# One five-column matmul per row tile in the experts' token fetch, and a small reduction on VectorE

## The chip, the core and the metric

The kernel runs on one core of one Trainium2 chip. The metric is the device time of that core in microseconds (us). The kernel before takes 3927.16 us, the median of three runs (3925.86 to 3930.93).

The engines are named as in the profile: PE is TensorE's matmul side and PEld its weight load, DVE is VectorE, ACT is ScalarE, POOL is GpSimd, SP is SyncE, which here only issues DMAs.

## The reference, cut to what matters

The program is two blocks one after the other. The first block has two layers; each ends in a mixture of experts over 1024 tokens of 1024 features. Every expert chooses its own 128 tokens:

```
aff = softmax(xn @ w_router)                  # [1024 tokens, 16 experts]
g, idx = top_k(aff.T, 128)                    # each expert's 128 tokens and their affinities
xg = xn[idx]                                  # their rows, [16, 128, 1024]
hid = silu(xg @ w_gate) * (xg @ w_up)         # 1024 -> 768
y = (hid @ w_down) * g                        # 768 -> 1024
h = h + zeros.at[idx].add(y)
```

All of it is in float32 accuracy: a matrix product is done as three products of a high and a low half.

## The kernel before

**The stage.** Each of the two layers runs the 16 experts in a stage of about 460 us (955 to 1420 us and 2102 to 2575 us). An expert's three matrices (9 MB) come from DRAM in six units of 128 x 3072: two each for gate, up and down. A unit is loaded by SP to `mwr`, its high half `mwh` is made on ACT (L130, three pieces of 128 x 1024), and its low half `mwl = mwr - mwh` on DVE or, for every sixth unit (down's first), on POOL (L134). There are three `mwh` and three `mwl` buffers, so a unit's halves can be made when the unit three places earlier has been used up on PE. PE multiplies 48 times for gate, 48 for up and 36 for down. Down's first unit feeds 18 matmuls, six to each piece of 1024; the third and fourth of each six read `mwl`.

**Around an expert.** `fetch` (L1190) finds the expert's tokens: DVE builds a one-hot matrix `oh` (tokens x slots, eight row tiles, L1195), PE multiplies it with the columns `lrhs` (token number in two parts, affinity in three), and the sums stand in a PSUM tile `idx`. The two parts of the token number are added in PSUM by a second matmul on the same one-hot tile. DVE then casts the number to an integer (`idx`, L1202) and adds the affinity's three parts (`gsc`, L1210), and POOL gathers the rows (`xg`, L1212). `tokens` (L1215) transposes the rows on PE in two groups of four (`xgT`), of which ACT and DVE make `xgh` and `xgl`. After gate and up, `hid` is formed by ACT (Silu, L1255) and DVE (L1256), transposed in two groups of three (`hT`) and split into `hh` and `hl`. `down` (L1269) is done one expert later; its result is scaled on ACT (`ye`, L1275) and scattered by POOL.

**PSUM.** Gate, up and down have two banks each. Everything small, that is `idx`, both `xgT` and both `hT`, shares two banks (tag `tp`): a third such tile waits until one of the two was read.

**The order.** It is written by a scheduler at build time, which plays the program through with its own estimates of time and puts the instructions of each engine in the order in which they came ready there (`high_priority` blocks first). On the chip every engine runs its list strictly in that order. The lists of the two layers' expert stages are the same.

Of the kernel before, what the change touches and what calls it, by code (L numbers as in the profile page):

```python
# [20 lines left out]
P = 128  # L21
# [55 lines left out]
class Kern:  # L77
# [10 lines left out]
    # -- small helpers --  # L88
# [9 lines left out]
    @contextmanager  # L98
    def staged(self, side=None, n=2048, bufs=2):
        """The ring that weights come in through: tiles [128, n]."""  # L100
        with self.pool("stage", bufs, side=side) as self.stage:
            self.stage_n = n
            yield

    def raw(self, k, n):
        """[128, k, n] of that ring."""
        return self.stage.tile([P, self.stage_n], F32, name="raw", tag="raw")[:, 0:k * n].rearrange("p (k n) -> p k n", k=k)
# [5 lines left out]
    def banks(self, ordered=False, **spec):  # L113
        """PSUM for one phase: tag=(banks a tile, tiles); ordered: in this order, else in that of use."""
# [21 lines left out]
    def rsqrt(self, v, n):  # L136
        """1/sqrt of v [P, n] (positive), on VectorE."""
# [16 lines left out]
    def bcast_row(self, pool, vec, n, name):  # L154
        """A DRAM vector [n] on every partition."""
        t = pool.tile([P, n], F32, name=name)
        self.nc.sync.dma_start(out=t, in_=vec.rearrange("(o n) -> o n", o=1).broadcast_to([P, n]))
        return t

    def columns(self, pool, rows, name):  # L160
        """DRAM row blocks [(n, 128) APs] -> [128, sum n], one column a row."""
# [19 lines left out]
    def to_T(self, xn, hi, lo, t, tags=("tp", "tp")):  # L181
        """xn [128 t, 1024 d] -> columns t of hi/lo [128, 8, T]."""
# [7 lines left out]
    def mm3(self, ps, wh, wl, uh, ul, kt, n=1024, first=True, last=True):  # L190
        """ps [M, n] += sum over k tiles of w^T u; w(k) gives [K, M] APs, u(k) gives [K, n] APs."""
# [8 lines left out]
def load_w(K, pool, W, c0, n, kt, name, lo_eng="dve", tag=None):  # L200
    """W [kt*128, C] columns c0:c0+n -> hi, lo [128, kt, n]."""
# [12 lines left out]
def weight_blocks(K, pool, W, c0, n, lo_eng="dve", bufs=2, tag=""):  # L214
    """Yields hi, lo [128, 8, 128] of the 128-column blocks of W [1024, C] from column c0."""
# [13 lines left out]
def range_reduced_sin(K, pool, out, z, b, fr, n):  # L229
    """out = sin(fr * (z + b)) for z [64, n] in PSUM."""  # L230
# [15 lines left out]
class Mixed:  # L246
    """A layer's transposed output in DRAM, in pieces of 128 rows and 512 tokens."""
# [5 lines left out]
    def store(self, k, src):  # L253
        """Rows k * 128 .. + 128 from src [128, T]."""
# [3 lines left out]
    def load(self, out, k0, k1, t):  # L258
        """out [128, KT, 128], its entries k0 .. k1: those row blocks of token tile t."""
# [7 lines left out]
class Hyena:  # L267
    """Layer 0's mixer: projections, implicit filters, long convolutions as real DFT products."""
# [25 lines left out]
    def load_forward(self, pool):  # L294
        """The matrices of the forward transform alone."""
# [3 lines left out]
    def load_inverse(self, pool):  # L299
        """Those of both transforms and those of the inverse one."""  # L300
# [7 lines left out]
    # folds of a [128, 1025] row block z (z[:, 1024] = 0); cos and sin sources may differ  # L308
# [33 lines left out]
    def to_freq_in(self, pool, f0, f1):  # L342
        """Folded rows of two channel tiles -> transposed hi/lo pieces, (class, j) -> [128, 512] views."""
# [15 lines left out]
    def forward(self, zt, emit):  # L359
        """emit(index 0..7, psum [128, 512] = C|S of 256 channels)."""  # L360
# [33 lines left out]
    def filter_mlp(self, sn, h2s):  # L394
        """The filters' hidden features [feature, t], hi over lo."""
# [26 lines left out]
    def stream_block(self, cb, wh, wl, uh, ul, wk):  # L422
        """Projected stream block cb [128 c, t] with its three-tap convolution, to DRAM."""
# [10 lines left out]
    def filters(self, h2s, zp, inverse):  # L434
        """The spectra of all filters, to DRAM; meanwhile the inverse transform's matrices."""
# [136 lines left out]
    def conv_out(self, g, o, z, Y, gate, wk, mixT):  # L572
        K, nc, mh, ml, ih, il = self.K, self.nc, self.mh, self.ml, self.ih, self.il
        V = nc.vector
        for ci in range(2):
# [21 lines left out]
            # unfold  # L597
# [81 lines left out]
def first_norm(K, pool, src, g, hi, lo, dst=None, each=None, bufs=8, gp=None, x0=None):  # L679
    """rms_norm of DRAM rows src [n*128, D] with gain g, transposed and split (and to DRAM dst); each(t) follows tile t.  # L680

    x0: the first 128 rows, if they are on chip."""
# [31 lines left out]
def accurate_exp(K, pool, x, n):  # L714
    """In-place exp of x [P, n] <= 0 on VectorE (float32 accuracy)."""
# [16 lines left out]
class Mem:  # L732
    """Memory cross-attention of one layer."""
# [7 lines left out]
    def load(self, pool):  # L741
        """Keys and values that were left in DRAM."""
# [12 lines left out]
    def kv(self, pool, mt, wp, mem):  # L755
        """Keys and values from the memory (hi, lo); pool holds what the attention needs."""
# [29 lines left out]
    def key_pair(self, pool, ps, n, name):  # L786
        """Two heads' K^T (64 partitions each) in PSUM -> [hi; hi] and [lo; lo] a head."""
# [13 lines left out]
    def queries(self, pool, w, uh, ul, tag="mm"):  # L801
        """qs [hi; lo] (the other way round for the odd head) of two heads; w their columns' hi, lo."""
# [11 lines left out]
    def attend(self, wk, mixT, row0, pair, qs, tg, pk=None):  # L814
        """Heads 2 pair and 2 pair + 1, token tiles 2 tg and 2 tg + 1."""
# [24 lines left out]
def scores(K, out, qs, k2, kl2):  # L840
    """out [128 t, n keys] = q k^T from the stacked halves."""
# [9 lines left out]
def softmax_rows(K, pool, ps, G):  # L851
    """ps [128, N] scores of G softmaxes a row -> probabilities [128, N] float32."""
# [16 lines left out]
def exp_rows(K, pool, ps, sm):  # L869
    """ps [128, n] scores of one softmax a row -> their exponentials under the row's maximum; the sums to sm."""  # L870
# [8 lines left out]
def columns_to_rows(K, ps, v):  # L879
    """ps [64, n * 128] (PSUM): column j of v [128, n] along the free dim, the same on each partition."""  # L880
# [4 lines left out]
def pT(K, prob, ph, pl, tt, pool=None, off=()):  # L885
    """prob's transpose, split, as columns of token tile tt of ph, pl; blocks of four key tiles in off are split from a copy on Pool."""
# [16 lines left out]
def out_heads(K, pool, ph, pl, kv, dst, tag="tp", sums=None):  # L903
    """dst (DRAM [64, n]) = V^T P^T (over sums [128, n / 128]); kv lists (index of ph, [hi | lo] values [128, 128])."""
# [26 lines left out]
class Moe:  # L931
# [14 lines left out]
    def out_weights(self, pool, rp, W, ks):  # L946
        """Row tiles ks of W, split."""
# [9 lines left out]
    def mix_out(self, mixT, W, xsrc):  # L957
        """h = x + mix @ W, its norm, the affinities, a token tile at a time.

        The mixer's last rows come last; the pools lie where its memory is free early."""  # L960
# [31 lines left out]
    def route_tile(self, wk, h, t, project):  # L992
        """Token tile t: h, its norm and its affinities; the last tile in halves, for the sake of what waits for it.

        The logits are four sums over two row blocks each, side by side in the array's columns."""
# [44 lines left out]
    def affinities(self, t):  # L1040
        """Those of token tiles t, t + 1 from the scaled logits."""
# [12 lines left out]
    def fall(self, src, s):  # L1054
        """Bitonic rows [n, 2 s] of src in falling order."""
# [12 lines left out]
    def larger(self, top, n):  # L1068
        """The larger halves of rows i and n + i of top [2 n, 128], sorted."""
# [7 lines left out]
    def joined(self, a, b):  # L1077
        """The 128 largest of two falling lists, sorted."""
# [4 lines left out]
    def pair_list(self, q):  # L1083
        """The 128 largest affinities a row of token tiles 2 q, 2 q + 1, in falling order: halves are sorted, then joined."""
# [17 lines left out]
    def route(self, pool):  # L1102
        """Slots [128 t, 8, 16] (minus 1000; 0 or more where a token is not chosen) and the matrices that list them."""
# [3 lines left out]
        with K.pool(name="rt", bufs=1, side="right") as rp:  # L1107
# [34 lines left out]
            # token number in two exact parts, affinity in three  # L1142
# [4 lines left out]
            nc.gpsimd.tensor_copy(out=rhs[:, :, :, 0], in_=iot[:, 0])  # L1147
# [3 lines left out]
            for j in range(3):  # L1151
                V.tensor_copy(out=rhs[:, :, :, 1 + j], in_=cur)
                if j < 2:
                    V.tensor_tensor(out=res, in0=cur, in1=rhs[:, :, :, 1 + j], op=OP.subtract)
                    cur = res
# [7 lines left out]
    def load(self, W, k0, n, c):  # L1163
        """Rows p * kt + k0 .. + n of every partition's run of W [kt * 128, c], split."""
# [13 lines left out]
    def accumulate(self, ps, parts, xh, xl, W, c):  # L1178
        """ps [128, c] = x W over all the rows of W, 3072 elements of a partition's run at a time."""
# [10 lines left out]
    def fetch(self, wk, xk, e):  # L1190
        """Expert e's token numbers, affinities and token rows."""
# [6 lines left out]
        for t in range(NT):  # L1198
            K.mm(ps[:, 0:4], oh[:, t], self.rhs[:, t, e, 0:4], t == 0, False)
            K.mm(ps[:, 0:1], oh[:, t], self.rhs[:, t, e, 4:5], False, t == NT - 1)  # L1200
        idx = wk.tile([P, 1], I32, name="idx", tag="idx", bufs=4)
        V.tensor_copy(out=idx, in_=ps[:, 0:1])  # L1202
# [1114 lines left out]
```

## Time and profile before

| | |
|---|---|
| median of three runs | 3927.16 us |
| span of the profiled execution | 3930.2 us |
| highest of the three runs | 3930.93 us |
| PE, DVE, ACT, POOL busy | 91%, 73%, 52%, 40% of the span |
| chain that ended last | PE 53%, DVE 13%, POOL 7%, ACT 4%, DMA 3% |
| mean granted TensorE clock | 0.953 of 2.4 GHz |
| DMA | 603.62 MB, mean 154 GB/s |

The profiled execution's span is 3.0 us above the median and 0.7 us under the highest of the three runs. In the profile's rows a group such as `mwl<-mwr,mwh` names the tile written and the tiles read; `x3` means three instructions in a row; a bracket tells how long the engine was idle before and what ended that idle time.

### The profile page before, as it was taken

To read this page: it belongs to the slowest core of one execution; us is meant where nothing else is said; L and a number is where in the kernel's file an instruction comes from. 1 tells how busy PE (TensorE), PEld (TensorE's weight loads), DVE (VectorE), ACT (ScalarE), POOL (GpSimd) and SP (SyncE) were. 2 spreads that over 40 slices of the span, in tenths; PEclk is the share of its full clock that TensorE was granted. 3 is DMA by queue.
4 is the path that set the end of the run, shared out by engine and by line. 5 is a ranking of instruction groups with operands and counts; after the bars stand their busy time and mean duration, and the time that the engine had idled before them with its cause. 6 is when DMAs were issued, how large, how long until landed. Compare 5 with 4: busy or idle time off the path is not lost.

```text
span 3930.2 us, 52452 instructions
## 1 busy us (share of the span) xinstructions
PE 3572.0 (91%) x19469; PEld 3034.8 (77%) x19469; DVE 2882.4 (73%) x4751; ACT 2047.2 (52%) x3063; POOL 1562.0 (40%) x1227
## 2 busy tenths in 40 slices
PE   7997999994999979899886999989998999999998
PEld 6885878773988979777765988978786877778777
DVE  6547878778888789777687988776476667765675
ACT  4333532233767754789634767745584245545430
POOL 2004745532443422244342543313351049774710
PEclk9998999897999999999997999999999999999999
DMA  4223333463999951000355999951114312222251
GB/s 152 96 82 109 116 129 114 132 233 143 363 356 353 369 178 37 11 10 12 100 203 216 367 348 353 350 151 53 38 39 133 99 56 91 70 75 76 91 176 65
DMA packets 205690, 603.62 MB, mean 154 GB/s; under 512 B 23095, under 2 KB 114073, under 8 KB 179834
## 3 DMA queue, kind: packets, MB, share of 16 engines
q1 hardware_dynamic: 193737, 558.58, 39.3%
q0 software_dynamic: 11696, 41.69, 4.1%
q8 instruction: 154, 2.52, 0.3%
q14 instruction: 103, 0.84, 0.1%
HBM read 503.59 MB, written 96.60 MB: 153 GB/s over the span
## 4 chain that ended last, share of the span: by engine, by line
PE 53%; DVE 13%; POOL 7%; ACT 4%; DMA 3%; issue 2%; SPq 0%; DVEq 0%; ACTq 0%; POOLq 0%
PE out L176 9%; PE gate L176 8%; PE xbc L176 5%; PE up L176 5%; PE down L176 5%; DVE mwl L134 2%; PE ov L176 2%; PE z L176 2%; PE gs L176 2%; PE pT L125 1%; PE as L176 1%; PE qk L176 1%; PE xr L176 1%; POOL csr L2048 1%; POOL csr L2047 1%
## 5 line engine op out<-in xcount | busy, mean ns | idle before, releaser
L134 DVE TENSOR_TENSOR mwl<-mwr,mwh 128x1024 fp32r<-128x1024 f32 x468 | 611.2, 1357 | 54.0 <-ACT mwh L130 52.9
L130 ACT ACTIVATE mwh<-mwr 128x1024 fp32r<-128x1024 f32 x576 | 562.7, 1050 | 48.6 <-PE up L176 24.5
L134 POOL TENSOR_TENSOR mwl<-mwr,mwh 128x1024 fp32r<-128x1024 f32 x108 | 295.0, 2759 | 311.2 <-ACT mwh L130 281.0
L915 POOL TENSOR_TENSOR oh<-oh,oh 64x256 f32<-64x256 f32 (+1 forms) x56 | 55.1, 984 | 401.2 <-ACT oh L914 386.7
L134 DVE TENSOR_TENSOR gpl<-pT,gph 128x512 fp32r<-128x512 f32 x168 | 110.5, 684 | 43.6 <-ACT gph L130 32.6
L1480 DVE SCALAR_TENSOR_TENSOR cv<-xbc,sdcols,cv 128x1021 f32<-128x1021 f32 (+2 forms) x72 | 91.9, 1276 | 65.8 <-ACT cv L1477 65.5
L125 PE MATMUL pT<-ident,prob 128*128 128x128 f32 x896 | 127.3, 278 | 13.5 <-DVE gpl L134 8.0
L873 DVE TENSOR_REDUCE mx<-gs 128x1 f32<-128x1024 f32 x96 | 116.8, 1218 | 30.9 <-PE gs L176 30.5
L176 PE MATMUL gate<-mwh,xgl 128*128 128x384 f32 x512 | 137.1, 349 | 0.3
L176 PE MATMUL gate<-mwl,xgh 128*128 128x384 f32 x512 | 135.6, 343 | 1.8 <-DVE mwl L134 1.6
L125 PEld LDWEIGHTS pT<-ident,prob 128*128 128x128 f32 x896 | 106.1, 142 | 39.4 <-ACT prob L875 6.8
L1212 POOL DMA_INDIRECT xg<-xn_d,idx x32 | 56.7, 1771 | 197.8 <-DVE gsc L1210 197.2
L176 PE MATMUL up<-mwl,xgh 128*128 128x384 f32 x512 | 131.7, 337 | 2.0 <-DVE mwl L134 2.0
L176 PE MATMUL gate<-mwh,xgh 128*128 128x384 f32 x512 | 133.3, 341 | 0.0
L176 PE MATMUL up<-mwh,xgh 128*128 128x384 f32 x512 | 132.1, 338 | 0.0
L176 PE MATMUL up<-mwh,xgl 128*128 128x384 f32 x512 | 131.2, 337 | 0.0
L176 PE MATMUL out<-pwh,pyl 128*128 128x512 f32 x384 | 122.4, 400 | 9.0 <-DVE pyl L134 6.7
L1287 POOL DMA_INDIRECT h_d<-ye,idx x32 | 74.2, 2319 | 135.3 <-ACT ye L1275 132.3
L134 DVE TENSOR_TENSOR wl<-raw,wh 128x1024 fp32r<-128x1024 f32 x71 | 111.2, 1567 | 22.4 <-ACT wh L130 22.2
L176 PE MATMUL down<-mwl,hh 128*128 128x512 f32 x384 | 123.2, 402 | 4.0 <-POOL mwl L134 3.9
L176 PE MATMUL out<-pwh,pyh 128*128 128x512 f32 x384 | 121.8, 398 | 0.0
L176 PE MATMUL out<-pwl,pyh 128*128 128x512 f32 x384 | 121.6, 397 | 0.0
(754 smaller groups left out, 11849.7 us busy)
## 6 DMA issues: line engine op xcount, KB each, us to landing
mwr<-in_exp_w_gate_dram SPq DMA_DIRECT2D x64, 1536.0 KB, 10.7
mwr<-in_exp_w_up_dram SPq DMA_DIRECT2D x64, 1536.0 KB, 10.4
mwr<-in_exp_w_down_dram SPq DMA_DIRECT2D x64, 1536.0 KB, 8.0
csr<-cs_d SPq DMA_DIRECT2D x32, 512.0 KB, 3.7
raw<-in_ssd_w_in_dram SPq DMA_DIRECT2D x15, 1024.0 KB, 5.4
k_d<-kev SPq DMA_DIRECT2D x54, 256.0 KB, 2.2
kt<-k_d SPq DMA_DIRECT2D x54, 256.0 KB, 2.8
raw<-in_hy_w_in_dram SPq DMA_DIRECT2D x10, 1024.0 KB
```

What stands on the lines that cost most here:

```text
L125: self.nc.tensor.transpose(out, in_, self.ident[:n, :n])
L130: nc.scalar.activation(out=hi, in_=src, func=AF.Copy)
L134: e.tensor_tensor(out=lo, in0=src, in1=hi.bitcast(F32), op=OP.subtract)
L176: self.nc.tensor.matmul(out=out, lhsT=lhsT, rhs=rhs, start=start, stop=stop)
L873: nc.vector.tensor_reduce(out=mx, in_=ps, axis=AX.X, op=OP.max, negate=True)
L915: nc.gpsimd.tensor_tensor(out=o2, in0=o2, in1=o, op=OP.add)
L1212: nc.gpsimd.indirect_dma_start(out=xg, out_offset=None, in_=self.xnD, in_offset=bass.IndirectOffsetOnAxis(ap=idx[:, 0:1], axis=0))
L1287: nc.gpsimd.indirect_dma_start(out=self.hD, out_offset=bass.IndirectOffsetOnAxis(ap=idx[:, 0:1], axis=0), in_=y, in_offset=None, compute_o ...
L1480: nc.vector.scalar_tensor_tensor(out=out[:, d:T], in0=ps[:, 0:T - d], scalar=cols[j], in1=out[:, d:T], op0=OP.mult, op1=OP.add)
L2047: G.tensor_tensor(out=m, in0=m, in1=per(self.cs[:, c, hs], P), op=OP.subtract)
L2048: G.tensor_tensor(out=m, in0=m, in1=self.msk.rearrange("p (o l) -> p o l", o=1).broadcast_to([P, 8, P]), op=OP.mult)
```

## The change

The columns of `lrhs` are put in another order, affinity first (columns 0 to 2) and then the token number's two parts (3 and 4). Each row tile's one-hot matrix is loaded and multiplied once with all five columns, instead of once with four and once with one. The two parts of the number, now in two PSUM columns, are added by a new DVE reduction into an SBUF tile `num`, and the cast (and, for the last two experts, the comparison `first`) reads `num` instead of PSUM. All other lines differ in comments alone; lines behind L1201 are numbered one higher.

```diff
@@ route @@
-            nc.gpsimd.tensor_copy(out=rhs[:, :, :, 0], in_=iot[:, 0])
+            nc.gpsimd.tensor_copy(out=rhs[:, :, :, 3], in_=iot[:, 0])
...
-                V.tensor_copy(out=rhs[:, :, :, 1 + j], in_=cur)
+                V.tensor_copy(out=rhs[:, :, :, j], in_=cur)
...
@@ fetch @@
         for t in range(NT):
-            K.mm(ps[:, 0:4], oh[:, t], self.rhs[:, t, e, 0:4], t == 0, False)
-            K.mm(ps[:, 0:1], oh[:, t], self.rhs[:, t, e, 4:5], False, t == NT - 1)
+            K.mm(ps[:, 0:5], oh[:, t], self.rhs[:, t, e], t == 0, t == NT - 1)
         idx = wk.tile([P, 1], I32, name="idx", tag="idx", bufs=4)
-        V.tensor_copy(out=idx, in_=ps[:, 0:1])
+        num = wk.tile([P, 1], F32, name="num", tag="num", bufs=2)
+        V.tensor_reduce(out=num, in_=ps[:, 3:5], axis=AX.X, op=OP.add)
+        V.tensor_copy(out=idx, in_=num)
...
-        V.tensor_reduce(out=g, in_=ps[:, 1:4], axis=AX.X, op=OP.add)
+        V.tensor_reduce(out=g, in_=ps[:, 0:3], axis=AX.X, op=OP.add)
```

The scheduler answers to this with another order in both expert stages, on PE, DVE and ACT, from the first fetch on, and with small shifts in the stages behind them. Three places follow.

DVE at the start of each layer's experts, before: expert 0's one-hot matrix, its cast and its affinity, then the one-hot matrices of the next two.

```order
L1195 TENSOR_TENSOR oh_8819<-iotac,slot 128x1024
L1202 CAST idx<-idx 128x1
L1210 TENSOR_REDUCE gsc<-idx 128x1
L1195 TENSOR_TENSOR oh_8844<-iotac,slot 128x1024
L1195 TENSOR_TENSOR oh_8889<-iotac,slot 128x1024
```

The same place now.

```order
L1195 TENSOR_TENSOR oh_8819<-iotac,slot 128x1024
L1202 TENSOR_REDUCE num<-idx 128x1
L1211 TENSOR_REDUCE gsc<-idx 128x1
L1195 TENSOR_TENSOR oh_8838<-iotac,slot 128x1024
L1203 CAST idx<-num 128x1
L1195 TENSOR_TENSOR oh_8877<-iotac,slot 128x1024
```

The cast, for which POOL's gather of expert 0 waits, now stands behind the one-hot matrix of expert 1; `num` and `gsc`, which empty the PSUM tile, stand at once behind the matmuls.

ACT over one cycle of a late expert (12 to 14), from one Silu to the next, before. The `mwh` pieces behind `hid` are up's second unit and down's first.

```order
L1255 ACTIVATE hid<-gate 128x768
L130 ACTIVATE mwh<-mwr 128x1024 x6
L130 ACTIVATE xgh<-xgT 128x512 x2
L130 ACTIVATE mwh<-mwr 128x1024 x3
L130 ACTIVATE hh<-hT 128x384 x2
L130 ACTIVATE mwh<-mwr 128x1024 x3
L1275 ACTIVATE ye<-down,gsc 128x1024
L130 ACTIVATE mwh<-mwr 128x1024 x6
L1255 ACTIVATE hid<-gate 128x768
```

The same cycle now; it repeats word for word for experts 8 to 14. The twelve pieces behind `hid` are up's second unit, down's first (whose low half POOL makes), down's second and the next gate's first.

```order
L1256 ACTIVATE hid<-gate 128x768
L130 ACTIVATE mwh<-mwr 128x1024 x12
L130 ACTIVATE xgh<-xgT 128x512 x2
L130 ACTIVATE mwh<-mwr 128x1024 x3
L130 ACTIVATE hh<-hT 128x384
L1276 ACTIVATE ye<-down,gsc 128x1024
L130 ACTIVATE hh<-hT 128x384
L130 ACTIVATE mwh<-mwr 128x1024 x3
L1256 ACTIVATE hid<-gate 128x768
```

Up's second and down's first unit follow `hid` in both; the next expert's `xgh` has moved behind all of down's pieces.

PE where the next expert's rows are transposed, in a late expert before: inside down's first unit.

```order
L125 MATMUL xgT<-ident,xg 128x128 x4
L176 MATMUL down<-mwl,hh 128x512 x2
L176 MATMUL down<-mwh,hh 128x512 x2
L176 MATMUL down<-mwh,hl 128x512 x2
L125 MATMUL xgT<-ident,xg 128x128 x4
L176 MATMUL down<-mwl,hh 128x512 x2
L176 MATMUL down<-mwh,hh 128x512 x2
L176 MATMUL down<-mwh,hl 128x512 x2
L125 MATMUL hT<-ident,hid 128x128 x3
```

And now: behind all 36 matmuls of down, straight ahead of gate.

```order
L176 MATMUL down<-mwh,hl 128x512 x2
L176 MATMUL down<-mwl,hh 128x512 x2
L176 MATMUL down<-mwh,hh 128x512 x2
L125 MATMUL xgT<-ident,xg 128x128 x8
L125 MATMUL hT<-ident,hid 128x128 x3
L176 MATMUL gate<-mwh,xgl 128x384 x2
L176 MATMUL gate<-mwl,xgh 128x384 x2
```

Down now runs its 36 matmuls with nothing between them, and gate follows eight `xgT` and three `hT`.

## Rows read from the trace of the kernel before

**Rows 1.** Busy time by stage, layers 0 and 1: window, length, PE, PEld, DVE, ACT, POOL, PEclk.
```profile
1006.90:1381.60 374.70, 361.23 (x2096) 332.66 (x2095) 315.44 (x302) 271.52 (x310) 162.84 (x64) 0.99 0.96 362
...
2156.80:2531.70 374.90, 361.45 (x2097) 332.88 (x2096) 315.33 (x302) 271.53 (x310) 168.32 (x64) 0.99 0.95 362
```

**Rows 2.** Chain in layer 0: start, length, what; gates of experts 2, 8, 13, 15.
```profile
1007.39 1.56 PE gate L176 x9
...
1179.84 4.18 PE gate L176 x24
...
1326.59 0.40 PE idx L176 x16
1326.98 8.43 PE gate L176 x48
1335.41 8.32 PE up L176 x48
...
1381.78 8.32 PE gate L176 x48
```

**Rows 3.** Operations of the tile idx: durations min/median/max in ns, first and last start.
```profile
L176 PE MATMUL idx<-lrhs,oh x512: 163/164/188, 952.3 to 2476.9; 128*128 128x4 bf16 x86, 128*128 128x1 bf16 x85
...
L1210 DVE TENSOR_REDUCE gsc<-idx x32: 142/148/153, 953.0 to 2499.7; 128x1 f32<-128x3 f32 x32
```

**Rows 4.** Timeline at layer 0's first fetch: start, length, engine, line, operation.
```profile
952.95 0.16 DVE L1202 CAST idx<-idx 128x1 int32<-128x1 f32 x1 [0.69 <-PE idx L176]
...
953.09 1.22 DVE L1195 TENSOR_TENSOR oh<-iotac,slot 128x1024 bf16<-128x1024 f32 x1
953.98 1.41 POOL L1212 DMA_INDIRECT xg<-xn_d,idx  x1 [39.27 <-DVE gsc L1210]
```

**Rows 5.** Timeline of PE and clock at expert 6's first gate matmuls.
```profile
1118.34 0.68 PE L125 MATMUL xgT<-ident,xg 128*128 128x128 f32 x4 [1.75 <-DVE gsc L1210]
...
1121.70:1126.20 4.50, 4.50 (x16) 4.50 (x15) 3.83 (x4) 1.17 (x2) 0.38 (x1) 0.50 1.00 415
```

**Rows 6.** Chain around down, xgT and hT in layer 0.
```profile
1169.07 8.20 PE down L176 x36
...
1210.05 0.67 PE hT L125 x3
...
1214.19 0.39 PE hT L125 x3
...
1344.21 0.44 PE xgT L125 x4
...
1346.07 0.71 PE xgT L125 x4
```

**Rows 7.** Timeline of expert 9's up and expert 8's down: POOL, DVE, PE.
```profile
1224.72 2.81 POOL L134 TENSOR_TENSOR mwl<-mwr,mwh 128x1024 fp32r<-128x1024 f32 x1 [12.79 <-ACT mwh L130]
...
1227.49 5.74 POOL L134 TENSOR_TENSOR mwl<-mwr,mwh 128x1024 fp32r<-128x1024 f32 x2
...
1228.30 0.96 DVE L1256 TENSOR_TENSOR hid<-up,hid 128x768 f32<-128x768 f32 x1 [3.04 <-PE up L176]
1229.18 1.81 DVE L134 TENSOR_TENSOR mwl<-mwr,mwh 128x1024 fp32r<-128x1024 f32 x1
...
1230.91 3.39 DVE L134 TENSOR_TENSOR mwl<-mwr,mwh 128x1024 fp32r<-128x1024 f32 x1
...
1228.10 0.63 PE L176 MATMUL down<-mwh,hl 128*128 128x512 f32 x2
...
1233.28 0.73 PE L176 MATMUL down<-mwl,hh 128*128 128x512 f32 x2 [1.22 <-POOL mwl L134]
```

**Rows 8.** Timeline of POOL at expert 13's down.
```profile
1367.93 7.50 POOL L134 TENSOR_TENSOR mwl<-mwr,mwh 128x1024 fp32r<-128x1024 f32 x3 [9.45 <-ACT mwh L130]
```

**Rows 9.** Timeline of ACT at the last down but one of layer 0.
```profile
1408.32 1.11 ACT L1275 ACTIVATE ye<-down,gsc 128x1024 f32<-128x1024 f32 x1 [1.56 <-PE down L176]
1409.34 2.94 ACT L130 ACTIVATE mwh<-mwr 128x1024 fp32r<-128x1024 f32 x3
```

More of the change, by code (lines that the diff above doesn't have):

```diff
@@ L1151, in route @@
             for j in range(3):
-                V.tensor_copy(out=rhs[:, :, :, 1 + j], in_=cur)
+                V.tensor_copy(out=rhs[:, :, :, j], in_=cur)
                 if j < 2:
-                    V.tensor_tensor(out=res, in0=cur, in1=rhs[:, :, :, 1 + j], op=OP.subtract)
+                    V.tensor_tensor(out=res, in0=cur, in1=rhs[:, :, :, j], op=OP.subtract)
                     cur = res
@@ L1205, in fetch @@
             oh = xk.tile([P, P], F32, name="ohf", tag="ohf", bufs=2)
-            V.tensor_scalar(out=first, in0=ps[:, 0:1], scalar1=-1000.0, scalar2=None, op0=OP.add)
+            V.tensor_scalar(out=first, in0=num, scalar1=-1000.0, scalar2=None, op0=OP.add)
             V.tensor_scalar(out=oh, in0=self.iota, scalar1=first, scalar2=None, op0=OP.is_equal)
```

## The prediction

> **What bounds the kernel now.** I read the busy time by stage first. In the 374.7 us of layer 0 that hold experts 2 to 14, PE is busy for 361.2 us at a granted clock of 0.99, DVE for 315, ACT for 272, POOL for 163, and layer 1's stretch is alike to 0.2 us [rows 1]. So PE bounds these stages, and what is worked out for layer 0 is counted twice. Next the chain of waits: in this stage it is almost wholly PE's own list, so a matmul taken out shortens the time, and an idle PE lengthens it by all of the idle. The gate of expert 2 starts at 1007.39, that of expert 8 at 1179.84, that of expert 15 at 1381.78 [rows 2]: experts 2 to 7 take 172.45 us, 28.74 each, experts 8 to 14 201.94, 28.85 each. Last I read the timeline where PE's idle time stands, to see who ended it: rows 5 and 7, below.
>
> **What the matmuls cost.** A fetch's 16 small matmuls stand on the chain with 0.40 us, 25 ns apart [rows 2]. Single ones, half of them with four columns and half with one, last 163 ns at the least and 164 in the median [rows 3], so columns do not show in the price at this size. Taking away eight of sixteen saves 0.2 us per fetch. A five-column matmul is not in the trace. Below, eight of them cost 0.2 us; above, the nearest other form is `xgT`, 0.44 us for four [rows 6], by which eight cost 0.88 and a fetch loses 0.48 (32 fetches: +15 us). I take the lower, since the four-column row is nearest by far. Over 32 fetches that is −6.4 us if nothing else moved.
>
> **What the reduction costs.** `num` is of `gsc`'s form, a narrow sum from PSUM, 148 ns [rows 3]; cast and `gsc` together delay the next `oh` by 0.14 us (952.95 to 953.09) [rows 4], so 0.07 us each on DVE, which is not the bound. What can cost is the wait: the cast now waits for `num`, and behind the cast wait the `oh` and `mwl` of DVE's list, and POOL's gather. In the late experts the gather is needed a whole down later, so I take nothing there; if `num` had to wait behind an `oh`, 1.22 us [rows 4].
>
> **The first fetch of a layer.** Here the order puts the cast behind the next `oh`, while POOL has nothing else to do: its gather follows the cast directly, after 39 us of idle [rows 4]. So +1.22 for the `oh`, +0.07 for `num`, −0.2 for the matmuls: +1.1 us per layer, carried whole by PE, which waits for these rows. At best nothing, if PE waits for expert 0's weights instead. The fetches of experts 0 and 1 give −0.2 each beside it: −0.4.
>
> **Experts 2 to 7.** Their fetches give −1.2. More is to be had from the PSUM tile. Before, `idx` kept one of the two small banks until DVE came to the cast; at expert 6 `xgT` waited 1.75 us for `gsc`, and the gate behind it ran for 4.50 us at a clock of 0.50 [rows 5]. Now `num` and `gsc` empty the bank ahead of the `mwl` pieces. The wait goes (1.75), and some of the 2.25 us that the low clock cost; another wait of that kind, for `xgl`, takes its place at one expert by the new list. Bounds: −1.2 (only matmuls) to −8 (two such waits of 1.75 + 2.25 fewer, no new ones: 8.0). I take −4.5, the middle.
>
> **Experts 8 to 14.** Here the order turns into one fixed cycle, which I add up along PE's list: gate 8.32 (the 48 matmuls of expert 15 without a wait), up 8.32 [rows 2], down 8.20 [rows 6], `idx` 0.2; from the start of the first `xgT` group to the next tile in its bank 1.86 (1344.21 to 1346.07) [rows 6], since the first `hT` must now wait until both `xgT` are read; that `hT` to the gate's start 0.67 [rows 6]; the second `hT`, 0.39 [rows 6]: 27.96 in all. That is 0.9 less than the 28.85 of before. But down now has nothing between its matmuls. At expert 8 it already ran in this way: it began at 1228.10, and POOL's third `mwl` piece ended at 1233.23; the first matmul that reads it started at 1233.28, 5.18 us in [rows 7]. Fourteen matmuls stand ahead of it, 14 x 8.20/36 = 3.19. So PE idles for 2.0 us, in every cycle, where before `xgT` and `hT` of the next expert filled part of it. 27.96 + 2.0 = 29.96; the last cycle lacks `idx`, 29.76; seven make 209.5, +7.6 us against 201.94.
>
> **The end of the experts.** ACT now splits expert 15's second down unit ahead of `ye` of expert 14, not behind it. That split takes 2.94 us, and `ye` waited 1.56 for PE [rows 9], so `ye` comes 1.4 us later and with it the scatter and what reads it. With one `hT` group of 0.4 moved into the last gate: +1.7. At best nothing of `ye` shows, since POOL's scatter of expert 15 is later still.
>
> **The sum.** Per layer −0.4 + 1.1 − 4.5 + 7.6 + 1.7 = +5.5; twice, +11 us. The durations are of an execution with a span of 3930.2; the page gives only that, 3.0 us above the median of 3927.16. I add the sum to the median: 3938 us. The other stages' small shifts I cost at nothing, with ±4 us as about half the bound of one layer's early experts.
>
> **Rivals.**
>
> *A, faster: the bank pays and POOL is in time.* The place is down's first unit, experts 8 to 14, and it decides there: if POOL's third piece ends within 3.19 us of down's start, PE never waits, and the cycle is 27.96. Per layer −0.4 + 1.1 − 4.5 − 6.4 + 1.7 = −8.5, in all −17: 3910 us. For it: the smaller tiles of PSUM are freed earlier everywhere. Against it: rows 7, where POOL, starting at 1224.72, 3.38 us before down, would have to do in 6.6 us what took it 8.5. The Trainium skill speaks for it in one point: in "Trainium Kernel Development and Optimization", section Best Practices, consistent bubbles are said to be a sign that SBUF or PSUM ran out, and freeing the bank would then be worth more than the matmuls. By rows 5 that holds at one expert.
>
> *B, no change: POOL undisturbed.* POOL's three pieces take 7.50 us where DVE does nothing beside them [rows 8], not 8.5. Begun 3.38 us ahead of down they end 4.12 us in, and PE idles 0.95. The cycle is 28.9, as long as before: seven, the last without `idx`, make 202.2, +0.2; per layer −0.4 + 1.1 − 4.5 + 0.2 + 1.7 = −1.9, in all −4: 3923 us. For it: DVE's pieces move too, and its `hid`, which stands ahead of them, waits for up's end. Against it: at expert 8 `hid` stood ahead of them as well, and DVE's pieces of 1.81 and 3.39 us then lay beside POOL's third [rows 7]. By the Trainium skill ("SBUF — State Buffer", section Who interferes with whom) DVE work with two SBUF inputs and a POOL instruction that reads SBUF exclude each other for a whole instruction, and who issues first goes first. Rows 7 fit that: the DVE piece beside POOL's took 3.39. If POOL's third piece issues first, the rule gives B's price, if DVE's does, the forecast's.
>
> *C, much slower: the clock.* An idle of 2 us at down and the wait for `xgl` ahead of `hT` stand in each late cycle. If PE's clock falls at them as at expert 6, each cycle adds the 2.25 us that 4.50 us at 0.50 cost [rows 5]: 14 x 2.25 = 31 on top of the forecast, 3969 us. For it: at expert 6 a shorter idle of 1.75 stood close before the fall. Against it: at expert 8 the waits of rows 7 stand in a stretch whose mean clock is 0.99 [rows 1], so an idle of this size alone did not do it. The Trainium skill's "TensorE: Matmul & The Clock Gate", section HAM oscillation, describes such a loop, in which a wait in each turn throttles the clock anew; by it C would hold in every cycle or in none.
>
> **How the numbers follow.** Forecast 0.48, A 0.17, B 0.28, C 0.07. Differences under 0.2% (7.9 us: 3919.3 to 3935.0) count as no change, which is about what a measurement of this kernel can tell. A lies wholly on the faster side, and of B a little (0.03): faster 0.20. The rest of B and the lower part of the forecast's own range (3931 to 3945), 0.07, are no change: 0.32. Left for slower: 0.41 and C, 0.48. The range reaches down to A and up over the forecast with the fetch's upper bound (3938 + 15 = 3953): 3909 to 3954; that leaves out half of A and C.
>
> **What will show it.** Right: the gates of experts 8 to 15 stand 29.96 us apart, with some 2 us of idle in each down that POOL's `mwl` ends, and 8 `idx` matmuls take 0.2 us; expert 2 to expert 8 takes about 168 us, with no `xgT` waiting for `gsc`; the first gather of a layer starts 1.1 us later after the one-hot matmuls. A shows as 27.96 us and no such idle, B as 28.9 and 1 us, C as clocks well under 0.99 in the late gates. Wrong altogether would be eight matmuls that take 0.4 us or more, or a difference that lies in stages outside the experts.

## The result and the profile after

The changed kernel takes 3954.98 us, the median of four runs (3953.69 to 3958.68), beside 3928.63 for the kernel before on the same chip: ratio 1.0064, 95% interval 1.0052 to 1.0075, so 20 to 30 us slower. The profiled execution's span is 3953.2 us, 23.0 above that of before. The direction and the main mechanism were as forecast; the loss is more than twice the forecast 11 us. Put on the 3927.16 us that the forecast started from, the ratio gives 3952 us, at the upper end of the range of 3909 to 3954; the median itself lies 1 us above it.

PE's own work became less, as the change says. This is the busy time by stage over experts 2 to 14 of layer 0, in the columns of [rows 1]:

```profile
1004.00:1386.10 382.10, 358.89 (x1996) 329.18 (x1995) 320.45 (x313) 271.15 (x310) 167.28 (x64) 1.00 0.95 357
```

PE is busy for 358.9 us, 2.3 less than in [rows 1], at a clock of 1.00, and yet the stretch takes 7.4 us longer: PE stands idle more. The chain of waits over one late cycle (from one expert's `xgT` to the next one's, experts 8 to 14) of layer 0 shows where (start, length, what):

```profile
1232.28 0.46 PE xgT L125 x4
...
1233.39 0.70 DVE xgl L134
...
1234.14 0.67 PE hT L125 x3
...
1238.29 0.38 PE hT L125 x3
...
1242.84 0.21 PE idx L176 x8
...
1251.39 5.75 POOL mwl L134 x2
...
1257.19 5.41 PE down L176 x22
1262.59 0.46 PE xgT L125 x4
```

From `xgT` to `xgT` it is 30.31 us. PE loses time at two places: ahead of `hT`, which waits for `xgl`, and in down, where the chain leaves PE for POOL's `mwl`. Eight `idx` matmuls take 0.21 us, half of the 0.40 of [rows 2]. The timeline of the same cycle, where down begins, answers to [rows 7]:

```profile
1248.62 8.51 POOL L134 TENSOR_TENSOR mwl<-mwr,mwh 128x1024 fp32r<-128x1024 f32 x3 [8.63 <-ACT mwh L130]
...
1252.01 0.62 PE L176 MATMUL down<-mwh,hl 128*128 128x512 f32 x2
...
1253.08 5.14 DVE L134 TENSOR_TENSOR mwl<-mwr,mwh 128x1024 fp32r<-128x1024 f32 x2
...
1253.89 0.30 PEld L176 LDWEIGHTS down<-mwl,hh 128*128 128x128 f32 x2 [0.30 <-POOL mwl L134]
...
1257.19 0.50 PE L176 MATMUL down<-mwl,hh 128*128 128x512 f32 x1 [1.64 <-POOL mwl L134]
```

Down starts 3.39 us after POOL. The first matmul that reads POOL's third piece starts 5.18 us into down, which is the figure of [rows 7]. New beside it is a shorter wait for POOL's second piece, 0.30 us.

The new forms cost what their nearest rows said (durations min/median/max in ns):

```profile
L176 PE MATMUL idx<-lrhs,oh x256: 165/166/187, 946.6 to 2498.7; 128*128 128x5 bf16 x128
L1202 DVE TENSOR_REDUCE num<-idx x32: 145/156/160, 947.0 to 2498.9; 128x1 f32<-128x2 f32 x32
```

The first gather of layer 0, in the columns of [rows 4]: the cast starts 1.28 us after `num`, behind an `oh`, and POOL waits for it.

```profile
947.02 0.16 DVE L1202 TENSOR_REDUCE num<-idx 128x1 f32<-128x2 f32 x1 [0.47 <-PE idx L176]
...
947.17 1.22 DVE L1195 TENSOR_TENSOR oh<-iotac,slot 128x1024 bf16<-128x1024 f32 x1
948.30 0.15 DVE L1203 CAST idx<-num 128x1 int32<-128x1 f32 x1
```

At expert 6 the wait of [rows 5] for `gsc` is gone, and one for POOL in down is new. The wait for `xgl` behind it is not new: the kernel before has it too, 2.10 us, between the two of rows 5. In the timeline of PE before:

```profile
1121.12 0.93 PE L125 MATMUL hT<-ident,hid 128*128 128x128 f32 x3 [2.10 <-DVE xgl L134]
```

The timeline now, and the window behind it (columns as in [rows 1]):

```profile
1108.14 0.73 PE L176 MATMUL down<-mwl,hh 128*128 128x512 f32 x2 [1.45 <-POOL mwl L134]
...
1116.70 0.67 PE L125 MATMUL hT<-ident,hid 128*128 128x128 f32 x3 [2.27 <-DVE xgl L134]
...
1117.50:1121.20 3.70, 3.70 (x14) 3.70 (x13) 3.61 (x4) 1.35 (x2) 0.16 (x1) 0.54 1.01 424
```

At the last down but one, ACT makes nine `mwh` pieces in a row and only then `ye`, where in [rows 9] the last three follow it. PE waits for this `ye` with the product `x` ahead of the last down. Timelines of ACT and PE now, and of PE before:

```profile
1405.74 8.63 ACT L130 ACTIVATE mwh<-mwr 128x1024 fp32r<-128x1024 f32 x9
...
1415.42 1.98 PE L176 MATMUL x<-ye,ohf 128*128 128x512 f32 x4 [2.16 <-ACT ye L1276]
...
1409.49 1.98 PE L176 MATMUL x<-ye,ohf 128*128 128x512 f32 x4 [1.21 <-ACT ye L1275]
```

The sum by the steps of the prediction, in us, from the starts of the first `idx` matmul, of the gates of experts 0, 2, 8 and 15, and from the end of the last down in both traces (after minus before):

| step | forecast, each layer | layer 0 | layer 1 |
|---|---|---|---|
| first fetch to gate 0 | +1.1 | +1.6 | +1.4 |
| gate 0 to gate 2 | −0.4 | +0.8 | −0.4 |
| experts 2 to 7 | −4.5 | −2.3 | −2.7 |
| experts 8 to 14 | +7.6 | +9.9 | +10.0 |
| gate 15 to the end of down | +1.7 | +1.9 | +1.9 |
| sum | +5.5 | +11.9 | +10.2 |

The two layers make 22.0 of the 23.0 us. The rest nearly cancels, by chance: −5.7 ahead of the first fetch, where the kernels differ only in the columns of `lrhs`, and +6.7 between and behind the stages. These parts also differ between executions: the first fetch started at 946.6 to 956.4 us over the profiled kernels below, which don't differ up to there in what they compute.

### The profile page after: what moved, and what is told of

The parts are those of the page before. It is cut to its first block, busy times and chain, and to the rows that moved or that the text cites. A ratio compares the mean times of both kernels' runs of the same rounds, so it can differ in the third digit from the quotient of the medians.

```text
span 3953.2 us, 51953 instructions
## 1 busy us (share of the span) xinstructions
PE 3564.4 (90%) x19213; PEld 3021.3 (76%) x19213; DVE 2892.8 (73%) x4783; ACT 2046.7 (52%) x3063; POOL 1569.3 (40%) x1227
## 4 chain that ended last, share of the span: by engine, by line
PE 49%; DVE 14%; POOL 9%; ACT 4%; DMA 4%; issue 3%; SPq 0%; ACTq 0%; DVEq 0%; POOLq 0%
PE out L176 9%; PE gate L176 8%; PE xbc L176 5%; PE down L176 4%; POOL mwl L134 3%; PE up L176 3%; DVE mwl L134 2%; PE ov L176 2%; PE gs L176 2%; PE z L176 2%; PE pT L125 2%; ACT mwh L130 1%; PE as L176 1%; PE qk L176 1%; PE xr L176 1%
## 5 line engine op out<-in xcount | busy, mean ns | idle before, releaser
L134 DVE TENSOR_TENSOR mwl<-mwr,mwh 128x1024 fp32r<-128x1024 f32 x468 | 627.3, 1391 | 49.8 <-ACT mwh L130 46.8
L134 POOL TENSOR_TENSOR mwl<-mwr,mwh 128x1024 fp32r<-128x1024 f32 x108 | 306.0, 2863 | 277.8 <-ACT mwh L130 267.1
L130 ACT ACTIVATE xgh<-xgT 128x512 fp32r<-128x512 f32 (+1 forms) x68 | 35.8, 566 | 189.7 <-PE xgT L125 189.3
L176 PE MATMUL down<-mwh,hl 128*128 128x512 f32 x384 | 122.3, 397 | 0.0
```

The source lines that it names most:

```text
L130: nc.scalar.activation(out=hi, in_=src, func=AF.Copy)
L134: e.tensor_tensor(out=lo, in0=src, in1=hi.bitcast(F32), op=OP.subtract)
L176: self.nc.tensor.matmul(out=out, lhsT=lhsT, rhs=rhs, start=start, stop=stop)
```

## The experiments

**Theory:** the loss belongs to the order that the scheduler wrote for the late experts, 36 matmuls of down in a row with `xgT` behind them; the change's own instructions are slightly cheaper than before. **Rivals:** the five-column matmul, the chain `num` to cast, or the early emptied PSUM tile costs the time itself. Ratios are to the kernel before on the same chip, with 95% intervals. The lengths, of layer 0, are from gate to gate of each trace.

| kernel | ratio | first fetch to gate 0 | experts 2 to 7 | experts 8 to 14 |
|---|---|---|---|---|
| before | 1 | 8.6 | 172.4 | 202.0 |
| changed | 1.0064 | 10.2 | 170.1 | 211.9 |
| e1 two matmuls, `num` | 1.0093 | 10.5 | 172.8 | 213.1 |
| e2 before with `num` | 1.0097 | 10.6 | 172.8 | 213.0 |
| e3 five columns, no `num` | 1.0063 | 8.5 | 169.3 | 212.0 |
| e4 changed, six `idx` | 0.9939 | 10.1 | 166.2 | 195.5 |
| e5 low products last | 1.0047 | 10.1 | 170.1 | 209.4 |
| e6 third piece on DVE | 1.0082 | 10.0 | 171.7 | 214.7 |
| e7 before, six `idx` | 0.9943 | 8.5 | 167.0 | 196.7 |
| e8 five columns, no `num`, six `idx` | 0.9935 | 8.4 | 166.7 | 195.7 |
| e9 before, two lines swapped | 1.0061 | 8.5 | 172.4 | 210.4 |
| e10 before, `num` behind the cast | 1.0006 | 8.6 | 172.7 | 202.5 |
| e11 e8 and six `gsc` | 0.9943 | 8.4 | 167.5 | 196.0 |

**e1: the matmuls given back.** The edit, on the changed kernel:

```diff
-            K.mm(ps[:, 0:5], oh[:, t], self.rhs[:, t, e], t == 0, t == NT - 1)
+            K.mm(ps[:, 0:4], oh[:, t], self.rhs[:, t, e, 0:4], t == 0, False)
+            K.mm(ps[:, 4:5], oh[:, t], self.rhs[:, t, e, 4:5], False, t == NT - 1)
```

> The changed kernel, but each row tile's one-hot matrix is again multiplied twice (columns 0 to 3, then column 4); the two number parts still stand in two PSUM columns and num adds them. The late experts' order is that of the changed kernel (36 down matmuls in a row, then eight xgT and three hT). Theory (the loss comes from the order that the early emptied PSUM tile brings): the POOL wait of 2.0 us in each late down stays, 256 matmuls at 25 ns come back: about 6 us above the changed kernel, 3961. Rival (the five-column matmul or its position is the cost): falls back to the kernel before or below it, 3928.

Measured: 3966.19 us, 1.0093 (1.0079 to 1.0108). The late cycle stays, and the five-column matmul is no cost but a gain; that rival falls. By the ratios the matmuls add 11 us and not the 6 that were worked out. Experts 8 to 14 take 1.2 us more per layer, as worked out, but experts 2 to 7 take 2.7 more. At expert 6 the granted clock is 0.50 for 6.8 us here (window, columns as in [rows 1]), 3.7 us at 0.54 in the changed kernel; with PE busy for 5.8 and 3.7 of them, that is about 1.2 of the 2.7:

```profile
1117.50:1124.30 6.80, 5.80 (x19) 5.80 (x20) 5.41 (x7) 2.34 (x3) 4.97 (x2) 0.50 1.00 412
```

**e2: only the early emptying.** On the kernel before:

```diff
-        V.tensor_copy(out=idx, in_=ps[:, 0:1])
+        num = wk.tile([P, 1], F32, name="num", tag="num", bufs=2)
+        V.tensor_copy(out=num, in_=ps[:, 0:1])
+        V.tensor_copy(out=idx, in_=num)
```

> The kernel before (two matmuls, number added in PSUM) with one copy more: DVE copies the number from PSUM to num, and the cast reads num. Theory: emptying the tile early is enough to bring the late cycle with its POOL wait, so about 6 us above the changed kernel, 3961, though no matmul is changed and one 0.07 us copy per fetch is added. Rival (copy and cast cost only their own 32 x 0.07 us): 3931, within noise of the kernel before.

Measured: 3969.44 us, 1.0097 (1.0082 to 1.0111). One small copy per fetch, which takes about 0.15 us by itself, makes the kernel 37 us slower, more than the some 30 that were expected. Its chain of waits has the late cycle:

```profile
1257.82 5.74 POOL mwl L134 x2
...
1263.60 5.40 PE down L176 x22
```

**e3: the five columns alone.** On the changed kernel, with no `num` between:

```diff
-        V.tensor_reduce(out=num, in_=ps[:, 3:5], axis=AX.X, op=OP.add)
-        V.tensor_copy(out=idx, in_=num)
+        with nc.allow_low_precision(reason="whole numbers"):
+            V.tensor_reduce(out=idx, in_=ps[:, 3:5], axis=AX.X, op=OP.add)
...
+            num = wk.tile([P, 1], F32, name="num", tag="num", bufs=2)
+            V.tensor_copy(out=num, in_=idx)
```

The last two added lines are for the last two experts alone, whose comparison `first` reads `num`.

> The changed kernel without num: the reduction writes the integer idx itself, straight from PSUM, as the cast did before (for the last two experts a copy of idx makes the number that first needs). Experts 0 to 7 then stand in the order of the kernel before, the late experts still in 36 down matmuls in a row, but with both hT groups inside gate. Theory: experts 2 to 7 take 172.4 - 1.2 = 171.2 us, the late experts keep the POOL wait of 2.0 us but lose the 1.2 us wait of hT for xgl if it is no longer ahead of gate: 29.0 to 29.6 us a cycle; 3930 to 3940 in all. Rival (the reduction, not the order, costs): 3922, six below the kernel before.

Measured: 3954.25 us, 1.0063 (1.0046 to 1.0081); expected were 3930 to 3940. The first fetch is back at 8.5 us, so its loss was the cast's place behind `oh`. But the late experts take as long as with `num`: the wait for `xgl` did not go when `hT` moved into gate, the second `xgT` has it instead (the first `xgT` group starts at 1265.66, behind down).

```profile
1266.78 0.70 DVE xgl L134
...
1267.52 0.71 PE xgT L125 x4
```

So the early emptied tile is not needed for the loss either: in experts 8 to 14 the sums in `idx` are read 20 to 22 us behind their matmuls here, 17 to 24 us in the kernel before, 0.2 us in the changed one. Each half of the change alone leads to the long cycle.

**e9: no half of it.** On the kernel before, the cast is written behind `gsc` instead of ahead of it, with the same instructions:

```diff
-        V.tensor_copy(out=idx, in_=ps[:, 0:1])
...
         V.tensor_reduce(out=g, in_=ps[:, 1:4], axis=AX.X, op=OP.add)
+        V.tensor_copy(out=idx, in_=ps[:, 0:1])
```

> The kernel before with two lines of fetch swapped: gsc is written ahead of the cast; every instruction is the same. In the order gsc now goes ahead, the cast stays late and empties the bank late, and from expert 9 on down's 36 matmuls stand in a row with xgT behind them, as in the kernel with the reduction to integer. Theory (the loss belongs to this late order, whatever brings it): late cycles of 30 to 31 us, about 10 us a layer above the kernel before, tail 1.7: 3931 + 20 to 24, ratio 1.005 to 1.0065. Rival (the loss belongs to the five columns, num, or the early emptied bank): none of them is here, ratio 1.000.

Measured: 3956.01 us, 1.0061 (1.0049 to 1.0073), the whole loss of the change without any of its instructions. Its chain has POOL's wait and the second `xgT`'s:

```profile
1254.74 5.72 POOL mwl L134 x2
...
1266.95 0.70 DVE xgl L134
...
1267.70 0.71 PE xgT L125 x4
```

**e10: one DVE instruction more, and the order kept.** On the kernel before:

```diff
         V.tensor_copy(out=idx, in_=ps[:, 0:1])
+        num = wk.tile([P, 1], F32, name="num", tag="num", bufs=2)
+        V.tensor_copy(out=num, in_=idx)
```

> The kernel before with one more 128x1 DVE copy per fetch, from idx to num behind the cast, which nothing reads; PSUM is emptied when it was before, and the order of the late experts stays that of the kernel before. Theory: one more small DVE instruction per fetch costs nothing: ratio 0.999 to 1.001. Rival (the extra DVE instruction itself delays the halves that PE waits for): 32 x 0.07 us or more, and like the kernel with num early, 1.004 or above.

Measured: 3932.08 us, 1.0006 (0.9997 to 1.0014). With e2 it separates the instruction from the order: the same number of instructions, 1.0097 where it stands between PSUM and the cast, nothing that can be told from noise where it stands behind.

**e5: POOL's wait within the same order.** On the changed kernel, in `accumulate`, for down's first unit only:

```diff
-                for j, (x, w) in enumerate(((xl, wh), (xh, wl), (xh, wh))):
...
+            if c == D and k0 == 0:
+                jobs = [(k, xl, wh) for k in range(n)] + [(k, xh, wh) for k in range(n)] + [(k, xh, wl) for k in range(n)]
...
```

> The changed kernel, but within down's first unit the 12 matmuls that read mwh stand ahead of the 6 that read mwl, the sums are the same. The late experts' order on all engines stays; the first matmul that reads POOL's third piece has 16 matmuls ahead of it in place of 14. Theory (POOL's third piece ends last): its wait falls from 2.01 us by 2 x 0.228 to 1.55 us in each late cycle, 30.3 to 29.85, and the kernel by 14 x 0.46 = 6 us, to 3948. Rival (PE waits there for something else, or POOL starts later by as much): 2.0 us again, 3954.

Measured: 3950.99 us, 1.0047 (1.0031 to 1.0063), whose interval meets that of the change; the traces are clearer, with 209.4 us in place of 211.9 for experts 8 to 14, 2.6 less where 3.2 were expected (timeline of POOL and PE):

```profile
1251.52 8.65 POOL L134 TENSOR_TENSOR mwl<-mwr,mwh 128x1024 fp32r<-128x1024 f32 x3 [8.62 <-ACT mwh L130]
...
1254.91 1.55 PE L176 MATMUL down<-mwh,hl 128*128 128x512 f32 x6
1256.30 1.56 PE L176 MATMUL down<-mwh,hh 128*128 128x512 f32 x6
1257.70 1.10 PE L176 MATMUL down<-mwl,hh 128*128 128x512 f32 x4
1260.23 0.73 PE L176 MATMUL down<-mwl,hh 128*128 128x512 f32 x2 [1.43 <-POOL mwl L134]
```

The 16 matmuls now run without a gap, and the wait of 1.64 became 1.43. It fell by less than the two matmuls put ahead of it: POOL ends 5.26 us into down here (1260.17 − 1254.91), 0.14 later than in the changed kernel, and the gap of 0.30 for the second piece, gone too, had been part of the 2.0. The mechanism holds, the size is four fifths of what was expected.

**e6: POOL's third piece given to DVE.** On the changed kernel:

```diff
-            K.split(hi[:, s], lo[:, s], raw[:, s], lo_eng="pool" if self.units <= 3 or self.units % 6 == 3 else "dve")
+            K.split(hi[:, s], lo[:, s], raw[:, s], lo_eng="pool" if self.units <= 3 or self.units % 6 == 3 and j < 2 else "dve")
```

> The changed kernel with the third low piece of down's first unit made on DVE in place of POOL (DVE gets 32 x 1.4 us more in all); in the order xgT moves inside down, and hT stays ahead of gate. Theory: no POOL wait in down, late cycles of 27.2 to 28.4 us in place of 30.3, in all 14 x (1.9 to 3.1) less: 3911 to 3928, at or below the kernel before. Rival (DVE, busy for 320 of 382 us, becomes the bound and PE waits for its mwl instead): cycles of 29.5 or more, 3945 or above.

Measured: 3963.72 us, 1.0082 (1.0064 to 1.0100): a miss. POOL's wait did go, but PE gained nothing. The timeline of a late cycle, the window behind the wait and the same stretch of the cycle before, and the window of the late experts:

```profile
1271.50 0.71 PE L125 MATMUL hT<-ident,hid 128*128 128x128 f32 x3 [1.85 <-DVE xgl L134]
...
1272.20:1275.30 3.10, 3.10 (x12) 3.10 (x11) 3.10 (x4) 1.81 (x3) 3.10 (x1) 0.50 0.99 402
1241.50:1244.60 3.10, 3.10 (x11) 3.10 (x11) 3.10 (x4) 1.80 (x3) 3.10 (x1) 0.50 0.97 350
...
1180.00:1388.00 208.00, 196.90 (x1047) 183.06 (x1046) 169.81 (x168) 143.72 (x162) 83.66 (x27) 0.94 0.93 341
```

The order moved too: the eight `xgT` stand inside down, 12 of its matmuls behind them, and DVE makes `xgl` behind two `mwl` pieces. `hT` waits for `xgl` for 1.85 us instead of 0.96, and behind it the gate runs at a granted clock of 0.50, that is at 1.2 GHz, for 3 us; over all late cycles the mean is 0.94, where the changed kernel has 1.00. So a cycle of 30.7 us in place of 30.3: 1.9 saved at POOL, 0.9 lost to the longer wait and about 1.5 to the clock. The rival was near in one point, since it is DVE that ends the wait, by `xgl` and not by `mwl`; the clock was in neither expectation.

**e4, e7, e8 and e11: six buffers of `idx`.** On the changed kernel (e4), on the kernel before (e7), and on the kernel of e3 (e8; with six `gsc` too: e11):

```diff
-        idx = wk.tile([P, 1], I32, name="idx", tag="idx", bufs=4)
+        idx = wk.tile([P, 1], I32, name="idx", tag="idx", bufs=6)
```

> The changed kernel with six buffers of idx in place of four: the cast of expert e no longer waits until POOL's scatter of expert e-4 has landed, so the gather starts a half gate earlier, and in the order xgT stands inside up or down and hT behind two matmuls of down's first unit. Theory: PE waits neither for POOL in down nor for xgl ahead of hT: late cycles of 27.4 to 27.9 us instead of 30.3, experts 2 to 7 about 167 us; 3954 - 2 x (17 to 20 + 3) = 3908 to 3914. Rival (the number's extra step and the later first gather are what costs): no change from the changed kernel, 3954.

> The kernel before (two matmuls, no num) with six buffers of idx in place of four. Theory: the order is that of the changed kernel with six buffers, so late cycles of about 28.1 us (27.9 + 0.2 for eight matmuls more), and the first gather is 1.1 us a layer earlier: ratio to the kernel before about 0.995, 4 us above the changed kernel with six buffers. Rival (it is the change that makes the bank's early release possible): 1.000.

> Six buffers of idx, five-column matmuls, and the reduction writes idx straight from PSUM, without num. Theory: the good order of the changed kernel with six buffers, without its late first gather (1.4 us a layer): ratio to the kernel before 0.992 to 0.994, 0 to 5 us below the changed kernel with six buffers. Rival (num helps to free the bank): slower than that kernel by 5 us or more.

> Six buffers of idx and of gsc, five-column matmuls, the reduction writes idx straight from PSUM. Theory: idx and gsc go together, early; late cycles of 27.9 us as with six idx buffers alone: ratio to the kernel before 0.992 to 0.994. Rival (the release of gsc is a wait of its own): below 0.992.

Measured: 3906.52 us, 0.9939 (0.9925 to 0.9953); 3910.69, 0.9943 (0.9926 to 0.9960); 3906.90, 0.9935 (0.9917 to 0.9953); 3908.95, 0.9943 (0.9931 to 0.9956). All four beat both kernels, by 0.6% against before and 1.2% against the change, and can't be told apart from each other by their times. A late cycle of e4 in the chain:

```profile
1219.03 0.97 DVE hid L1257
...
1220.04 1.08 PE hT L125 x6
1221.12 1.41 PE down L176 x6
1222.52 0.20 PE idx L176 x8
1222.72 0.55 PE xgT L125 x4
1223.27 5.58 PE down L176 x24
1228.86 0.44 PE xgT L125 x4
1229.29 0.93 PE down L176 x4
...
1246.91 0.97 DVE hid L1257
```

From `hid` to `hid` it is 27.88 us. `hT`, `idx` and the first `xgT` stand in down's first unit, and POOL is in time: from 1200 to 1368 us PE's one wait is that for `hid` (us in total, times, longest):

```profile
PE hT L125 <- DVE hid L1257: 3.5, 6, 0.6
```

What the two buffers moved is the cast. DVE's timeline of the changed kernel, where the `idx` matmuls end at 1243.05, and of e4, where they end at 1222.72:

```profile
1266.28 0.15 DVE L1203 CAST idx<-num 128x1 int32<-128x1 f32 x1
...
1223.97 0.15 DVE L1203 CAST idx<-num 128x1 int32<-128x1 f32 x1
```

It stands 23.2 us behind the sums in the one and 1.3 us in the other, and the gather follows it. The same late cycle of e7, with 16 `idx` matmuls:

```profile
1223.26 0.40 PE idx L176 x16
...
1251.37 0.40 PE idx L176 x16
```

That is 28.11 us, 0.2 more: within nearly the same order (in e7 the second `xgT` stands behind the last four matmuls of down, not ahead of them), the change's matmuls are worth their rows. e4 against e7 is therefore the change with most of its reordering taken out: −1.2 us in experts 8 to 14, −0.9 in 2 to 7, +1.5 at the first fetch.

## Why the prediction was right, and where it was mis-sized

**Which way, and where.** Right: PE stayed the bound, the early experts got faster, the late ones slower, and PE waits for POOL's `mwl` in each of the seven late downs, 5.18 us in, as forecast. The idle of 2.0 us in down came out as 0.30 for POOL's second piece and 1.64 for its third.

**Experts 8 to 14, +7.6 forecast, +9.9 measured.** The cycle is 30.3 us, not 29.96. `xgT` to `hT` took the forecast 1.86, `idx` 0.21, the two `hT` 0.67 and 0.38. Down is the term that was too small: 10.58 us (1252.01 to 1262.59) where 8.20 + 2.0 were taken. The 22 matmuls behind the wait take 5.41, not 22/36 of 8.20, which is 5.01. A down without a wait [rows 6] was the wrong row for what follows one: a pair of matmuls that has waited takes 0.73 [rows 7], one that has not 0.63; and the 8.20 us leave out the first 0.16 us of down, in which the last matmul of up still ran (down's first matmul starts at 1168.91, the chain counts from 1169.07). The third part was not to be seen beforehand. In the changed kernel down is slower also where it does not wait (chain):

```profile
1163.31 8.39 PE down L176 x36
```

That is 0.19 more than in rows 6, so 0.12 for 22 matmuls, and the three make the 0.4. A single matmul of down takes 394 ns in the median, 389 before; gate and up are as before. This pace is not what the loss comes from: e10 has the 8.39 at a ratio of 1.0006, and e3 has the 8.20 of before at 1.0063. What sets it was not tried.

**Experts 2 to 7, −4.5 forecast, −2.3 and −2.7 measured.** This is the step that failed. The bank was to pay 3.3 us and the matmuls 1.2. e1, with the early emptied bank and 16 matmuls, takes 172.8 us, no less than the kernel before: in the order that came with it, the bank pays nothing. The wait of 1.75 for `gsc` went, but one of 1.45 for POOL came at the same expert. The wait for `xgl` there was in the trace before, 2.10 us, and stayed with 2.27; the prediction's reading of rows 5 left it out, took the `gsc` wait alone for what the slow clock followed, and so counted on more than the bank could give. Against e1 the matmuls give 2.7: 1.2 of their own time and about 1.2 by the shorter slow clock; the waits at expert 6 differ too. By the 0.19 us above, down's slower pace takes up to 1.1 us back over six experts, an estimate.

**First fetch and end.** +1.1 became +1.6 and +1.4, of which e3 and e8 show the cause: without the cast behind `oh` the stretch is 8.4 to 8.5 us. +1.7 became +1.9, but that it came so close is partly luck. `ye` does stand behind the `mwh` pieces, as the order said; PE, which waits for it with `x`, waits 0.95 us longer and not 1.4, the moved `hT` takes its 0.4, and most of the rest is the slower pace of two downs, which was in no term. The gain of the fetches of experts 0 and 1 shows in layer 1 alone.

**The rivals.** A (bank pays, POOL in time) and B (POOL's third piece undisturbed by DVE) did not come: POOL took 8.51 us for three, with DVE's pieces of 5.14 for two beside it. C did not come in the changed kernel, whose clock is 1.00 over the late stretch. Its case rested on expert 6, where not one wait of 1.75 but two, of 1.75 and 2.10, stood before the fall. It was a real mechanism nevertheless: e6 shows it, with the `xgl` wait 0.9 us longer. The Trainium skill ("TensorE: Matmul & The Clock Gate", section HAM oscillation) describes a loop in which a wait in each turn throttles the clock anew; the trace of e6 agrees, with the stretch at 0.50 in one cycle after the other and the mean of 0.94, and that of the changed kernel, with a shorter wait ahead of the same `hT`, does not show it. The waits of the page's example, 3 to 5 us, are longer than the 1.85 us of e6.

**What was not among the cases.** I took the late order for a consequence of the early emptied PSUM tile. e3 and e9 bring an order as slow without it, e9 without any change in the instructions. How the scheduler comes to either order is not shown by any trace; shown is that the change, e2, e3 and e9 lead to the long cycle, e10 does not, and two more `idx` buffers lead to a shorter one whether the change is made or not.

## What to carry to other kernels

Where a scheduler writes the order, time the edit and the new order apart: a line that keeps the instructions (e9) or a buffer that lifts a wait (e4 against e7) tells what the edit itself is worth, here a few us at most against 25 from the order. When matmuls that covered the making of a late piece move away, read from the trace when that piece is done. A buffer of a few bytes that holds up the start of a long chain is worth a look first. Here four `idx` tiles let the scheduler place the cast only behind the scatter of four experts earlier; on the chip that scatter had landed at 1250.40, 15.9 us before the cast at 1266.28, so it was the written place that cost, not a wait.

## What the runs showed of the chip

A wait of 1.64 us in down and one of 0.96 ahead of `hT`, in every late cycle of the changed kernel, left the granted clock at 1.00. One wait of 1.85 ahead of `hT` in e6, behind 12 matmuls of down, was followed by 3 us at 0.50, with a mean of 0.94 over the late cycles. At expert 6 waits of 1.75 and 2.10 close together were followed by 0.50 in the kernel before, waits of 1.45 and, ending 8.6 us later, 2.27 by 3.7 us at 0.54 in the changed kernel; but waits of 1.12 and, ending 8.6 us later, 2.09 by no fall in e3 (timeline of PE, then the window around it):

```profile
1120.43 0.67 PE L125 MATMUL hT<-ident,hid 128*128 128x128 f32 x3 [2.09 <-DVE xgl L134]
...
1119.00:1126.00 7.00, 5.57 (x33) 5.57 (x34) 6.33 (x8) 4.20 (x7) 2.09 (x2) 1.00 1.00 410
```

So the length of a wait alone does not tell whether the clock falls: 1.85 was enough in e6, and 2.09 was not in e3. What else decides was not tried.

Three pieces of POOL's low half took 8.51 us beside two of DVE's, which took 5.14, and 7.50 us where DVE did nothing beside them [rows 8].
